# A streaming-encoder step on one core: gathers at a closer pace in the last trunk group, expert weights in the trunk's slots, row buffers from the expansion's, and a lead of two keys

## The chip, the cores and the metric

The kernel runs on one core of a Trainium2 chip. The metric is the device time of one execution in microseconds (us), the median over runs. A profiled execution has a span, from its first to its last instruction, that is a little shorter than its time. TensorE (PE) does the matrix products, VectorE (DVE) and ScalarE (ACT) the elementwise work, GpSimd (POOL) issues the indirect gathers and some stores, and SyncE (SP) issues the other transfers. Each engine and each issuing queue works through its own instructions in a fixed order.

## The reference

One layer of a hybrid encoder runs over 1152 rows of 1024 numbers: 1024 rows of one prompt and 8 × 16 rows of sampled streams. With the rows in tiles of 128 there are nine: tile 0 holds the samples, tiles 1 to 8 the prompt.

```
h = rmsnorm(x);  z = h @ w_in                      # 1024 x 10240
branch A: gelu(u) * (tril(W_s) rmsnorm(gelu(v)) + b_s), in chunks of 128 positions
branch B: retention, 4 heads, rotary q and k, a decayed state carried from tile to tile
x = x + (sigmoid(gA) * (yA @ w_proj_a) + sigmoid(gB) * (yB @ w_proj_b)) @ w_out
t = rmsnorm(x)
q = t @ w_query                                    # 8 heads of 2 x 128
top 16 of 128 keys on each half, then the top 16 of the 256 sums: 8 x 16 = 128 experts a row
w = softmax(the 16 values)
x = x + sum over the 128 experts:  w * gelu(t . eu[expert]) * ev[expert]
y = rmsnorm(x)
```

There are 128 × 128 = 16384 experts, each with a row of 1024 numbers in `expert_u` and another in `expert_v`. All values are float32.

## The kernel before, in words

**Two ways through the expert layer.** Six of the nine tiles (0, 1, 2, 6, 7, 8, the list `GATHER`) fetch the rows of their experts. For each of the 128 expert slots of a tile, one indirect transfer brings to each of the 128 partitions the pair (u row, v row) of its own expert: 8 KB a partition, 1 MB a gather, 768 gathers in all. DVE forms the dot product with `tx` (line 794), ACT applies gelu and the weight (lines 799 and 800), and DVE adds the weighted v row to `acc` (line 804). The other three tiles (3, 4, 5, the list `DENSE`) go through all experts. For each first key `e` of 128, the 128 experts of that key give S = tT · eu[e] (line 1017), then gelu and a product with a dense weight table `pt` (line 1022, the result is `g`), then a product with ev[e] (line 1029) that accumulates over all keys in six PSUM banks `res`.

**The trunk.** The tiles pass through the trunk in three groups, [0, 1], [2, 3, 4, 5], [6, 7, 8] (`trunk`, called at lines 968 to 973). Each group takes the same 128 weight units of 512 KB, in the order of the list `order`, through `take` (lines 137 to 160). In the first two groups each unit is split into two parts for a three-product matmul. There the raw units lie partly in the row buffers `gat` described below (line 121). The last group uses units as they are, in nine slots: three buffers each of the names `wraw`, `whi` and `wlo`. A load is issued as soon as the slot's last user has been taken (`room`).

**Side work.** While the trunk is traced, two lanes of side work are traced between its steps. One lane (`prepare`) picks the top keys of a tile as soon as its group is through the trunk, and for a dense tile expands the choice into the table `pdr` in DRAM, 32 chunks a tile, through tiles `ab` and `st` of the pool `ex` (lines 844 to 896). The other (`gather_all`, `gather`) hands out gathers. Both lanes and the trunk carry a time in model units: a matmul pass over n columns counts n / 2400 (`mm_us`), a gather counts `PACE[0]`, which is 5.0 in the trunk and 3.4 in the dense stage, and the lane that is furthest behind goes next (`run_side`, `advance`). So `PACE` sets how many gathers are traced among how much trunk work. A gather may be traced only for a tile whose group has left the trunk. So tiles 0, 1 and 2 can be gathered during the trunk and tiles 6, 7 and 8 only after it.

**What sets the order.** The traced order is a priority, not the final order. A scheduler that models the engines gives each engine the first instruction in this order that is ready, so side work can move ahead of the trunk where its buffers allow. `tc.high_priority` moves the dense stage's own instructions forward against the gathers. Once each engine's order is fixed, the chip runs it in that order.

**Buffers of the gathers.** A gather takes one of five buffers `gat` in the pool `peer`. `AHEAD` is how many gathers may be queued before the oldest is dotted, three in the trunk. After the trunk, the pools of the trunk weights and the expansion are closed, and in that memory new pools open: `gx` with three more row buffers `gax` (the lead then becomes six) and `dw` with four buffers `eu` and five `ev` for the dense weights (`fetch`, lines 997 to 1002). Keys 0, 1 and 2 are fetched at the start, then key e + 3 while key e is worked on. The table of the weights is read in 16 blocks of eight keys, two buffers `pt`, at the start of each block. The product with ev of key e − 1 follows S of key e: a lead of one key.

**The end.** After the last key the three dense tiles add `res` to their rows, normalise and store (lines 1038 to 1046), and the lane of gathers runs to its end.

Of the kernel before, what the change touches and what calls it, by code (L numbers as in the profile page):

```python
# [8 lines left out]
F32 = mybir.dt.float32  # L9
# [4 lines left out]
AF = mybir.ActivationFunctionType  # L14
# [34 lines left out]
EC = 4  # L49
LT = 16  # L50
BE = 8

@with_exitstack
def step_kernel(ctx: ExitStack, tc: tile.TileContext, x, state, wall, wst, bs, rows, vec, cst, smp, cosd, sind, euv,
# [4 lines left out]
    dr = ctx.enter_context(tc.tile_pool(name="dr", bufs=1, space=bass.MemoryType.DRAM))  # L61
    peer = ctx.enter_context(tc.tile_pool(name="peer", bufs=1))
    act = ctx.enter_context(tc.tile_pool(name="act", bufs=1))
    trunk_sb, trunk_ps = ExitStack(), ExitStack()
    wp = trunk_sb.enter_context(tc.tile_pool(name="wp", bufs=2))
    gp = trunk_ps.enter_context(tc.tile_pool(name="gp", bufs=2, space=bass.MemoryType.PSUM))
    sp = trunk_ps.enter_context(tc.tile_pool(name="sp", bufs=4, space=bass.MemoryType.PSUM))

# [25 lines left out]
    for g in range(len(GROUPS)):  # L94
# [10 lines left out]
            order += [U_IN + 2 * (32 + cb), U_IN + 2 * (32 + cb) + 1, U_PA + 2 * cb, U_PA + 2 * cb + 1]  # L105
        order += [U_OUT + i for i in range(8)] + [U_Q + i for i in range(16)]
    per = len(order) // len(GROUPS)
    NRAW, NPART, NBK = 3, 3, 2
    GB = 5
    MIX = 3  # L110
# [26 lines left out]
    def take():  # L137

        n = wst_["take"]
        wst_["take"] += 1  # L140
        while wst_["split"] < min(n + 3, plain_from):
            s = wst_["split"]
            while wst_["load"] < min(s + n_raw(wst_["load"]), plain_from):
                l = wst_["load"]
                raws[l] = load(l)
                wst_["load"] += 1
            parts[s] = [wp.tile([P, 4, 256], F32R, name=n, bufs=NPART) for n in ("whi", "wlo")]
            for r in homes[1:]:
                rings[r].append(s)
            split(parts[s], raws.pop(s))  # L150
            wst_["split"] += 1
        if wst_["split"] == plain_from:
            while wst_["load"] < len(order) and room(wst_["load"], n):
                l = wst_["load"]
                t = wp.tile([P, 4, 256], F32, name=homes[l % 3], bufs=NPART)
                nc.sync.dma_start(t, wall[order[l]])
                rings[homes[l % 3]].append(l)
                parts[l] = [t]
                wst_["load"] += 1
        return order[n], parts.pop(n)  # L160

    def products(w, a):
        return [(w[0], a[0])] if len(a) == 1 else [(w[0], a[0]), (w[1], a[0]), (w[0], a[1])]
# [474 lines left out]
    def query(gi, pl, tl, nt, T, tT, rs, unit):  # L638
        def scores(h, qh):
            for i, t in enumerate(tl):  # L640
                ps = sp.tile([P, 2, P], F32, name="sps")
                for c in range(2):
                    mm(ps[:, c], qh[:, c, i * P:(i + 1) * P], sk[c], start=True, stop=True)
                st = pl.tile([P, 2, P], F32, name="st", bufs=2 * nt)
                nc.scalar.activation(st, ps, AF.Copy, scale=rs[:, i:i + 1])
                st = st.rearrange("p a b -> p (a b)")
                if t in EARLY:
                    top_keys(t, h, st)
                else:
                    store(ssp[t][:, h], st, 1)  # L650

        prev = None
        ahead = front(gi + 1, pl) if gi + 1 < len(GROUPS) else turn_dense(pl)
        next(ahead, None)
        for h in range(PH):
            qh = pl.tile([P, 2, T], F32, name="qh", bufs=2)
            unit = unit or gemm_f(tT, T, U_Q + 2 * h)
            nc.scalar.copy(qh, (yield from unit))
            unit = None
            if prev:  # L660
                scores(*prev)
            if h > 1:
                next(ahead, None)
            prev = (h, qh)
            yield 0.5 * nt
        scores(*prev)
        yield 0.5 * nt
        for _ in ahead:
            pass


    AHEAD = [3]
    more = []
    PACE = [5.0]
    BOOST = [100]
    AB = 2
# [112 lines left out]

    queue, rows_ = [], []  # L790

    def dot(t, j, b):
        d = T_[t]
        nc.vector.tensor_tensor_reduce(out=b[:, :D], in0=b[:, :D], in1=d["x"], op0=OP.mult, op1=OP.add,  # L794
                                       scale=1.0, scalar=0.0, accum_out=d["s"][:, j:j + 1])
# [6 lines left out]
    def add(t, j, b):  # L802
        d = T_[t]
        nc.vector.scalar_tensor_tensor(d["acc"], b[:, D:], d["s"][:, j:j + 1], d["acc"], op0=OP.mult, op1=OP.add)  # L804
        if j == HK - 1:
            tmp = more[0].tile([P, 2 * D], F32, name="jn") if more else peer.tile([P, 2 * D], F32, name="gat", bufs=GB)
            out_norm(d["acc"], tmp, t)
            del T_[t]

# [16 lines left out]
    def gather(t):  # L826
        d = T_[t]
        d["x"] = peer.tile([P, D], F32, name="tx")
        nc.sync.dma_start(d["x"], tsp[t])
        d["acc"] = peer.tile([P, D], F32, name="acc", bufs=2)  # L830
        nc.sync.dma_start(d["acc"], xsp[t])
        for j in range(HK):
            rows_.append(j)
            if more and len(rows_) % (GB + more[1]) >= GB:
                b = more[0].tile([P, 2 * D], F32, name="gax", bufs=more[1])
            else:
                b = peer.tile([P, 2 * D], F32, name="gat", bufs=GB)
            nc.gpsimd.indirect_dma_start(out=b, out_offset=None, in_=euv,  # L838
                                         in_offset=bass.IndirectOffsetOnAxis(ap=d["idx"][:, j:j + 1], axis=0))
            queue.insert(0, (t, j, b))  # L840
            gathered()
            yield PACE[0]
# [54 lines left out]

    def out_norm(acc, tmp, t):

        nc.sync.dma_start(tmp[:, D:], row_bcast(rows, 2))  # L900
        final_norm(acc, tmp[:, :D], tmp[:, D:], t)

    def final_norm(acc, junk, g, t):
        r = peer.tile([P, 1], F32, name="rfin", bufs=2)
# [7 lines left out]
    def prepare():  # L912

        left, wait = list(GATHER), list(DENSE)
        while left or wait:
# [5 lines left out]
            elif due is not None:  # L921
                yield from chain(topk_units("p", due), expand(due))
                wait.remove(due)
                expanded.add(due)
            else:
                yield None

# [36 lines left out]
        flush()  # L964
        run_side(tm)

    ex_sb = ExitStack()
    for gi in range(len(GROUPS)):
        if gi == len(GROUPS) - 1:
            ex = ex_sb.enter_context(tc.tile_pool(name="ex", bufs=1))  # L970
        for c in trunk(gi):
            advance(c)
        ready.update(GROUPS[gi])
# [3 lines left out]
    while len(expanded) < len(DENSE):  # L977
        tm += 1.0
        run_side(tm)
    dense_sb = ExitStack()  # L980
    wd = dense_sb.enter_context(tc.tile_pool(name="dw", bufs=1, side="right"))
    ex_sb.close()
    trunk_sb.close()
    trunk_ps.close()
    GX = 3
    gx = ctx.enter_context(tc.tile_pool(name="gx", bufs=1))
    dp = dense_sb.enter_context(tc.tile_pool(name="dp", bufs=1))
    dps = ctx.enter_context(tc.tile_pool(name="dps", bufs=1, space=bass.MemoryType.PSUM))
    more.extend([gx, GX])
    AHEAD[0] += GX  # L990

    outs = [(n, j) for j in range(2) for n in range(len(DENSE))]
    res = {o: dps.tile([P, 512], F32, name=f"res{o[0]}{o[1]}") for o in outs}
    eu, ev, G = {}, {}, {}
    pt = None

    def fetch(e):
        if e < NKEYS:
            eu[e] = wd.tile([P, D], F32, name="eu", bufs=4)
            nc.sync.dma_start(eu[e], eud[e].rearrange("p k e -> p (k e)"))  # L1000
            ev[e] = wd.tile([P, D], F32, name="ev", bufs=5)
            nc.sync.dma_start(ev[e], evd[e])

    PACE[0] = 3.4
    hp = ExitStack()
    hp.enter_context(tc.high_priority(DP))
    for e in range(3):
        fetch(e)
    for e in range(NKEYS + 1):
        if e < NKEYS:  # L1010
            if e % BE == 0:
                pt = dp.tile([P, TD // LT, BE, LT], F32, name="pt", bufs=2)
                nc.sync.dma_start(pt.rearrange("p c e t -> p c (e t)"), pdr[e // BE])
            ps = dps.tile([P, TD], F32, name="S", bufs=2)
            w = eu.pop(e)
            for k in range(KD):
                mm(ps, w[:, k * P:(k + 1) * P], tT[:, k], start=k == 0, stop=k == KD - 1)  # L1017
            fetch(e + 3)
            a = G[e] = dp.tile([P, TD], F32, name="g", bufs=4)
            nc.scalar.activation(a, ps, AF.Gelu_apprx_tanh)  # L1020
            r16 = lambda z: z.rearrange("p (c t) -> p c t", t=LT)
            nc.vector.tensor_tensor(r16(a), r16(a), pt[:, :, e % BE], op=OP.mult)  # L1022
            hp.close()
            advance(8 * 4 * mm_us(TD))
            hp.enter_context(tc.high_priority(DP))
        if e:
            g, w = G.pop(e - 1), ev.pop(e - 1)
            for n, j in outs:
                mm(res[n, j], g[:, n * P:(n + 1) * P], w[:, 512 * j:512 * j + 512], start=e == 1, stop=e == NKEYS)  # L1029
            hp.close()  # L1030
            advance(len(outs) * 4 * mm_us(512))
            hp.enter_context(tc.high_priority(DP))
    hp.close()
    dense_sb.close()
    dz = ctx.enter_context(tc.tile_pool(name="dz", bufs=len(DENSE)))
    grow = dz.tile([P, D], F32, name="grow", bufs=1)
# [92 lines left out]
```

## Time and profile before

| | us |
|---|---|
| median of 3 runs | 3996.11 (3987.49 to 3996.43) |
| the profiled execution | 3993.61 |
| its span | 3991.9 |
| PE busy | 3564.0 (89%) |
| DVE busy | 3095.6 (78%) |
| POOL busy | 1139.9 (29%) |
| DMA | 1291.31 MB, 323 GB/s over the span |

The views give times from the span's start. A window row holds the window and its length, then busy time and number of instructions of each engine, the granted clock of PE as a share of full speed, the mean busy share of the 16 DMA engines and what they moved. A row of the timeline holds the start, the length, engine, line, operation, output and inputs with their shapes, the number of merged instructions, and in brackets how long the engine had been idle and what ended this. A group's row holds the count, the busy time, the mean in ns, the idle time before, and what ended most of it. A matmul of float32 shows as two records, so a dense key has 28: sixteen of S and twelve of `res`. A transfer's row holds its count, its size and the median time from issue to landing.

### The profile page before, as it was taken

To read this page: it belongs to the slowest core of one execution; us is meant where nothing else is said; L and a number is where in the kernel's file an instruction comes from. 1 tells how busy PE (TensorE), PEld (TensorE's weight loads), DVE (VectorE), ACT (ScalarE), POOL (GpSimd) and SP (SyncE) were. 2 spreads that over 40 slices of the span, in tenths; PEclk is the share of its full clock that TensorE was granted. 3 is DMA by queue.
4 is the path that set the end of the run, shared out by engine and by line. 5 is a ranking of instruction groups with operands and counts; after the bars stand their busy time and mean duration, and the time that the engine had idled before them with its cause. 6 is when DMAs were issued, how large, how long until landed. Compare 5 with 4: busy or idle time off the path is not lost. (4 is left out here: it accounts for less than half of the span.)

```text
span 3991.9 us, 45577 instructions
## 1 busy us (share of the span) xinstructions
PE 3564.0 (89%) x15681; PEld 2456.4 (62%) x15681; DVE 3095.6 (78%) x5859; ACT 1364.9 (34%) x3291; POOL 1139.9 (29%) x812
## 2 busy tenths in 40 slices
PE   8999999999998889988999969989999999999930
PEld 6789978787888766766586734444444444444410
DVE  5566799999898789898731269989777777777777
ACT  4445634444434425556351212121111211121121
POOL 0000013333333311323200014444333343443443
PEclk9999999999999999999999989999999999999965
DMA  8766548999988976979743469999999999999997
GB/s 313 262 222 197 174 167 350 365 354 336 366 327 340 352 266 205 359 261 358 269 143 123 151 246 414 418 388 418 418 419 419 400 418 418 418 419 418 418 362 265
DMA packets 257817, 1291.31 MB, mean 323 GB/s; under 512 B 28336, under 2 KB 43440, under 8 KB 157232
## 3 DMA queue, kind: packets, MB, share of 16 engines
q0 software_dynamic: 121472, 847.30, 53.8%
q1 hardware_dynamic: 136112, 441.08, 29.8%
q8 instruction: 124, 2.03, 0.2%
q14 instruction: 109, 0.89, 0.1%
HBM read 1221.16 MB, written 67.11 MB: 323 GB/s over the span
## 5 line engine op out<-in xcount | busy, mean ns | idle before, releaser
L838 POOL DMA_INDIRECT gat<-in_euv_dram,idx x588 | 838.7, 1426 | 1738.8 <-DVE acc L804 1089.7
L804 DVE SCALAR_TENSOR_TENSOR acc<-gat,sdot,acc 128x1024 f32<-128x1024 f32 x588 | 752.1, 1279 | 107.3 <-ACT sdot L800 103.1
L794 DVE CUSTOM_DVE_ANT_0 gat<-gat,tx 128x1024 f32<-128x1024 f32 x588 | 716.3, 1219 | 151.7 <-DMA gat<-in_euv_dram,idx 124.5
L1029 PE MATMUL res<-ev,g 128*128 128x512 f32 x1536 | 741.6, 612 | 100.3 <-DVE g L1022 100.1
L799 ACT ACTIVATE sdot<-sdot 128x1 f32<-128x1 f32 x768 | 154.6, 203 | 1781.4 <-DVE sdot L794 1779.9
L1017 PE MATMUL S<-h,eu 128*128 128x384 f32 x2048 | 724.0, 491 | 36.0 <-issue 29.6
L1017 PEld LDWEIGHTS S<-h,eu 128*128 128x128 f32 x2048 | 393.1, 192 | 383.8 <-issue 192.9
L1029 PEld LDWEIGHTS res<-ev,g 128*128 128x128 f32 x1536 | 293.6, 195 | 434.8 <-issue 223.3
L214 PE MATMUL gps<-whi,h 128*128 128x256 f32 x2688 | 518.3, 300 | 2.9 <-issue 1.2
L214 PEld LDWEIGHTS gps<-whi,h 128*128 128x128 f32 x2688 | 437.3, 193 | 23.4 <-issue 11.8
L838 POOL DMA_INDIRECT gax<-in_euv_dram,idx x180 | 259.8, 1443 | 602.6 <-DVE acc L804 299.8
L214 PE MATMUL gps<-wlo,h 128*128 128x256 f32 x1536 | 417.9, 310 | 4.4 <-DVE wlo L228 3.0
L198 PE MATMUL gps<-h,whi 128*128 128x256 f32 (+2 forms) x1520 | 405.6, 364 | 1.3 <-ACT whi L222 1.2
L198 PE MATMUL gps<-y,whi 128*128 128x256 f32 (+2 forms) x1168 | 308.8, 360 | 7.8 <-DVE y L228 3.0
L214 PEld LDWEIGHTS gps<-wlo,h 128*128 128x128 f32 x1536 | 294.7, 193 | 22.0 <-issue 9.0
L198 PEld LDWEIGHTS gps<-h,whi 128*128 128x128 f32 x1520 | 269.9, 192 | 57.6 <-ACT whi L222 1.4
L198 PE MATMUL gps<-h,wlo 128*128 128x256 f32 (+2 forms) x864 | 293.3, 379 | 6.7 <-DVE wlo L228 6.5
L804 DVE SCALAR_TENSOR_TENSOR acc<-gax,sdot,acc 128x1024 f32<-128x1024 f32 x180 | 230.7, 1282 | 61.8 <-ACT sdot L800 59.1
L794 DVE CUSTOM_DVE_ANT_0 gax<-gax,tx 128x1024 f32<-128x1024 f32 x180 | 219.9, 1222 | 44.3 <-DMA gax<-in_euv_dram,idx 43.4
L198 PEld LDWEIGHTS gps<-y,whi 128*128 128x128 f32 x1168 | 205.3, 192 | 49.9 <-DVE y L228 3.4
L228 DVE TENSOR_TENSOR wlo<-wraw,whi 128x1024 fp32r<-128x1024 f32 x172 | 209.2, 1216 | 30.8 <-ACT whi L222 30.5
L222 ACT CAST whi<-wraw 128x1024 fp32r<-128x1024 f32 x172 | 179.9, 1046 | 154.0 <-PE gps L198 91.9
(220 smaller groups left out, 4411.1 us busy)
## 6 DMA issues: line engine op xcount, KB each, us to landing
wraw<-in_wall_dram SPq DMA_DIRECT2D x214, 512.0 KB, 6.2
eu<-in_eud_dram SPq DMA_DIRECT2D x128, 512.0 KB, 8.1
ev<-in_evd_dram SPq DMA_DIRECT2D x128, 512.0 KB, 9.9
gat<-in_wall_dram SPq DMA_DIRECT2D x84, 512.0 KB, 4.7
pdr<-st POOLq DMA_DIRECT2D x24, 1024.0 KB, 6.9
pt<-pdr SPq DMA_DIRECT2D x16, 1536.0 KB, 10.8
wlo<-in_wall_dram SPq DMA_DIRECT2D x43, 512.0 KB, 4.7
whi<-in_wall_dram SPq DMA_DIRECT2D x43, 512.0 KB, 5.1
```

The source lines that it names most:

```text
L198: mm(ps[:, c, :T], x, y, start=kh == 0 and k == 0 and j == 0, stop=kh == nk - 1 and k == 3 and j == len(pr) - 1)
L214: mm(ps[:, i], y, x, start=kh == 0 and k == 0 and j == 0 and i % 2 == 0, stop=kh == 1 and k == 3 and j == len(pr) - 1 and last)
L222: nc.scalar.copy(parts[0], src)
L228: nc.vector.tensor_tensor(parts[1], src, parts[0].bitcast(F32), op=OP.subtract)
L794: nc.vector.tensor_tensor_reduce(out=b[:, :D], in0=b[:, :D], in1=d["x"], op0=OP.mult, op1=OP.add, scale=1.0, scalar=0.0, accum_out=d["s"][ ...
L799: nc.scalar.activation(d["s"][:, j:j + 1], d["s"][:, j:j + 1], AF.Gelu_apprx_tanh)
L804: nc.vector.scalar_tensor_tensor(d["acc"], b[:, D:], d["s"][:, j:j + 1], d["acc"], op0=OP.mult, op1=OP.add)
L838: nc.gpsimd.indirect_dma_start(out=b, out_offset=None, in_=euv, in_offset=bass.IndirectOffsetOnAxis(ap=d["idx"][:, j:j + 1], axis=0))
L1017: mm(ps, w[:, k * P:(k + 1) * P], tT[:, k], start=k == 0, stop=k == KD - 1)
L1029: mm(res[n, j], g[:, n * P:(n + 1) * P], w[:, 512 * j:512 * j + 512], start=e == 1, stop=e == NKEYS)
```

## The change

- The list of weight units goes on after the trunk: for 130 steps, unit ("u", e) for each key and unit ("v", e − 2) two steps later. `take` loads them through the same nine slots as the last trunk group's units. The pool `wp` stays open to the end, and `dw`, `eu`, `ev` and `fetch` are gone.
- `PACE` is 3.2 instead of 5.0 from the start of the last trunk group.
- When the last dense tile is expanded, the two buffers `st` of the expansion (8 KB a partition, as a gather's) join the five `gat` as row buffers, and `AHEAD` goes from 3 to 5. After the trunk one `gax` joins instead of three, and `AHEAD` is 6, as before. The scratch of a tile's last step is taken from `ab` and no longer from a row buffer or `jn`.
- The first block `pt` gets a pool of its own, opened in the last query stage, and is loaded from head 4 on if all is expanded, or after the trunk otherwise. Later blocks are loaded four keys ahead, in turns in two pools.
- The two PSUM tiles `S` are allocated ahead of the six `res`.
- The product with ev runs two keys behind S in place of one.

```
+LEAD = 2
...
+    for e in range(NKEYS + LEAD):
+        order += [("u", e)] * (e < NKEYS) + [("v", e - LEAD)] * (e >= LEAD)
...
-                nc.sync.dma_start(t, wall[order[l]])
+                nc.sync.dma_start(t, unit_of(l))
...
+    def unit_of(l):
+        if l < per * len(GROUPS):
+            return wall[order[l]]
+        kind, e = order[l]
+        if kind == "u":
+            return eud[e].rearrange("p (a k) e -> p a (k e)", a=4)
+        return evd[e].rearrange("p (k e) -> p k e", k=4)
...
+            if gi == len(GROUPS) - 1 and h >= 4 and not pts and len(expanded) == len(DENSE):
+                load_pt(pp[0], 0)
...
+    rings_ = [(peer, "gat", GB)] * GB
...
-            if more and len(rows_) % (GB + more[1]) >= GB:
-                b = more[0].tile([P, 2 * D], F32, name="gax", bufs=more[1])
-            else:
-                b = peer.tile([P, 2 * D], F32, name="gat", bufs=GB)
+            pool, name, bufs = rings_[len(rows_) % len(rings_)]
+            b = pool.tile([P, 2 * D], F32, name=name, bufs=bufs)
...
+                if not wait:
+                    rings_.extend([(ex, "st", 2)] * 2)
+                    AHEAD[0] += 2
...
         if gi == len(GROUPS) - 1:
-            ex = ex_sb.enter_context(tc.tile_pool(name="ex", bufs=1))
+            ex = ctx.enter_context(tc.tile_pool(name="ex", bufs=1))
+            PACE[0] = 3.2
...
-    more.extend([gx, GX])
-    AHEAD[0] += GX
+    rings_.append((gx, "gax", 1))
+    AHEAD[0] += 1
...
+    for e in range(2):
+        Ss[e] = dps.tile([P, TD], F32, name="S", bufs=2)
...
+    for e in range(NKEYS + LEAD):
         if e < NKEYS:
+            with tc.high_priority(DP):
+                if e % BE == BE // 2 and e // BE + 1 < NKEYS // BE:
+                    load_pt(pp[0] if e // BE % 2 else dp, e // BE + 1)
...
+                u, (w,) = take()
...
+        if e >= LEAD:
+            with tc.high_priority(DP):
+                u, (w,) = take()
...
+                g = G.pop(e - LEAD)
```

More of the change, by code (lines that the diff above doesn't have):

```diff
@@ L63, in step_kernel @@
     act = ctx.enter_context(tc.tile_pool(name="act", bufs=1))
-    trunk_sb, trunk_ps = ExitStack(), ExitStack()
-    wp = trunk_sb.enter_context(tc.tile_pool(name="wp", bufs=2))
+    trunk_ps, dense_sb = ExitStack(), ExitStack()
+    wp = ctx.enter_context(tc.tile_pool(name="wp", bufs=2))
     gp = trunk_ps.enter_context(tc.tile_pool(name="gp", bufs=2, space=bass.MemoryType.PSUM))
@@ L650, in scores @@
                     store(ssp[t][:, h], st, 1)
+        if gi == len(GROUPS) - 1:
+            pp.append(dense_sb.enter_context(tc.tile_pool(name="pp", bufs=1, side="right")))
         prev = None
@@ L669, in query, with load_pt @@
             pass
+    pp, pts = [], []
+    def load_pt(pool, n):
+        pts.append(pool.tile([P, TD // LT, BE, LT], F32, name="pt"))
+        nc.sync.dma_start(pts[-1].rearrange("p c e t -> p c (e t)"), pdr[n])
     AHEAD = [3]
-    more = []
     PACE = [5.0]
@@ L805, in add @@
         if j == HK - 1:
-            tmp = more[0].tile([P, 2 * D], F32, name="jn") if more else peer.tile([P, 2 * D], F32, name="gat", bufs=GB)
+            if len(rings_) > GB:
+                tmp = [ex.tile([P, D], F32, name="ab", bufs=AB) for _ in range(2)]
+            else:
+                tmp = peer.tile([P, 2, D], F32, name="gat", bufs=GB)
+                tmp = [tmp[:, 0], tmp[:, 1]]
             out_norm(d["acc"], tmp, t)
@@ L898, in out_norm @@
     def out_norm(acc, tmp, t):
-        nc.sync.dma_start(tmp[:, D:], row_bcast(rows, 2))
-        final_norm(acc, tmp[:, :D], tmp[:, D:], t)
+        nc.sync.dma_start(tmp[1], row_bcast(rows, 2))
+        final_norm(acc, tmp[0], tmp[1], t)
     def final_norm(acc, junk, g, t):
@@ L965, in advance @@
         run_side(tm)
-    ex_sb = ExitStack()
     for gi in range(len(GROUPS)):
         if gi == len(GROUPS) - 1:
-            ex = ex_sb.enter_context(tc.tile_pool(name="ex", bufs=1))
+            ex = ctx.enter_context(tc.tile_pool(name="ex", bufs=1))
+            PACE[0] = 3.2
         for c in trunk(gi):
@@ L979, in step_kernel @@
         run_side(tm)
[L980 to L983, printed above, removed]
     trunk_ps.close()
-    GX = 3
+    if not pts:
+        load_pt(pp[0], 0)
+    dg = ctx.enter_context(tc.tile_pool(name="dg", bufs=1))
     gx = ctx.enter_context(tc.tile_pool(name="gx", bufs=1))
@@ L988, in step_kernel @@
     dps = ctx.enter_context(tc.tile_pool(name="dps", bufs=1, space=bass.MemoryType.PSUM))
-    more.extend([gx, GX])
-    AHEAD[0] += GX
+    rings_.append((gx, "gax", 1))
+    AHEAD[0] += 1
     outs = [(n, j) for j in range(2) for n in range(len(DENSE))]
+    Ss = {}
+    for e in range(2):
+        Ss[e] = dps.tile([P, TD], F32, name="S", bufs=2)
     res = {o: dps.tile([P, 512], F32, name=f"res{o[0]}{o[1]}") for o in outs}
-    eu, ev, G = {}, {}, {}
-    pt = None
-    def fetch(e):
+    G = {}
@@ L998, in fetch @@
+    PACE[0] = 3.4
+    for e in range(NKEYS + LEAD):
         if e < NKEYS:
[L999 to L1023, printed above, removed]
-            advance(8 * 4 * mm_us(TD))
[L1025 to L1030, printed above, removed]
@@ new lines, in step_kernel @@
+            with tc.high_priority(DP):
+                if e % BE == BE // 2 and e // BE + 1 < NKEYS // BE:
+                    load_pt(pp[0] if e // BE % 2 else dp, e // BE + 1)
+                if e % BE == 0 and e:
+                    pts.pop(0)
+                ps = Ss.pop(e) if e in Ss else dps.tile([P, TD], F32, name="S", bufs=2)
+                u, (w,) = take()
+                assert u == ("u", e)
+                w = w.rearrange("p a b -> p (a b)")
+                for k in range(KD):
+                    mm(ps, w[:, k * P:(k + 1) * P], tT[:, k], start=k == 0, stop=k == KD - 1)
+                a = G[e] = dg.tile([P, TD], F32, name="g", bufs=4)
+                nc.scalar.activation(a, ps, AF.Gelu_apprx_tanh)
+                r16 = lambda z: z.rearrange("p (c t) -> p c t", t=LT)
+                nc.vector.tensor_tensor(r16(a), r16(a), pts[0][:, :, e % BE], op=OP.mult)
@@ L1031, in step_kernel @@
+            advance(8 * 4 * mm_us(TD))
+        if e >= LEAD:
+            with tc.high_priority(DP):
+                u, (w,) = take()
+                assert u == ("v", e - LEAD)
+                w = w.rearrange("p a b -> p (a b)")
+                g = G.pop(e - LEAD)
+                for n, j in outs:
+                    mm(res[n, j], g[:, n * P:(n + 1) * P], w[:, 512 * j:512 * j + 512], start=e == LEAD,
+                       stop=e == NKEYS + LEAD - 1)
             advance(len(outs) * 4 * mm_us(512))
-            hp.enter_context(tc.high_priority(DP))
@@ L1033, in step_kernel @@
-    hp.close()
     dense_sb.close()
```

## Prediction

> **What bounds the kernel now.** I read the slices first, then busy time by stage, counts of gathers by stage, the waits of PE and POOL, and last the timelines at the seams. Stages (columns: window, length; busy us and instruction count of PE, PEld, DVE, ACT, POOL; granted clock; DMA share; GB/s):
>
> ```profile
> 600.00:1390.00 790.00, 741.00 (x4144) 631.64 (x4143) 718.23 (x987) 348.10 (x770) 277.83 (x189) 0.97 0.92 349
> 1420.00:1990.00 570.00, 517.93 (x2197) 370.99 (x2196) 510.32 (x1432) 289.97 (x681) 143.78 (x107) 0.95 0.77 284
> 1990.00:2329.00 339.00, 339.00 (x1442) 241.97 (x1442) 95.85 (x352) 110.61 (x255) 9.96 (x9) 1.00 0.40 127
> 2329.00:2359.00 30.00, 0.39 (x4) 0.23 (x3) 21.87 (x101) 3.61 (x10) 5.57 (x6) 0.57 0.78 292
> 2440.00:3800.00 1360.00, 1262.51 (x3320) 633.30 (x3319) 1086.75 (x1639) 254.01 (x922) 561.70 (x394) 0.98 1.01 415
> 3836.00:3992.00 156.00, 0.00 (x0) 0.00 (x0) 117.03 (x149) 34.06 (x107) 61.18 (x38) 0.51 0.77 288
> ```
>
> The dense stage (2440 to 3800) runs with the DMA engines full at 415 GB/s. The end of the last trunk group (1990 to 2329) uses 127 GB/s, with DVE busy 96 of 339 us. After the dense matmuls come 156 us of gathers alone. The gathers by stage (POOL busy and count), the gap on POOL, and the seams on PE and DVE:
>
> ```profile
> 0.00:1420.00 1420.00, 301.20 (x208) 0.97 0.80 297
> 1420.00:1990.00 570.00, 122.97 (x90) 0.95 0.77 284
> 1990.00:2329.00 339.00, 1.77 (x2) 1.00 0.40 127
> 2329.00:3836.00 1507.00, 611.30 (x433) 0.96 1.01 412
> 3836.00:3992.00 156.00, 61.18 (x38) 0.51 0.77 288
> ...
> 1959.39 1.41 POOL L838 DMA_INDIRECT gat<-in_euv_dram,idx  x1 [1.12 <-DVE acc L804]
> 2118.76 1.15 POOL L868 DMA_DIRECT2D pdr<-st  x1 [14.33 <-ACT st L866]
> 2326.92 1.00 POOL L838 DMA_INDIRECT gax<-in_euv_dram,idx  x1 [207.01 <-PE gps L198]
> ...
> 1419.72 4.36 PE L198 MATMUL gps<-h,whi 128*128 128x384 f32 x13
> 2326.48 2.84 PE L643 MATMUL sps<-vc,qh 128*128 128x128 f32 x24
> 2358.93 13.14 PE L1017 MATMUL S<-h,eu 128*128 128x384 f32 x32 [29.61 <-issue]
> 3826.23 9.07 PE L1029 MATMUL res<-ev,g 128*128 128x512 f32 x14 [4.39 <-DVE g L1022]
> ...
> 3861.51 1.28 DVE L907 SCALAR_TENSOR_TENSOR dx<-dx,rfin,grow 128x1024 f32<-128x1024 f32 x1
> 3979.38 1.28 DVE L804 SCALAR_TENSOR_TENSOR acc<-gax,sdot,acc 128x1024 f32<-128x1024 f32 x1 [0.60 <-ACT sdot L800]
> 3982.40 1.28 DVE L804 SCALAR_TENSOR_TENSOR acc<-gat,sdot,acc 128x1024 f32<-128x1024 f32 x1 [0.60 <-ACT sdot L800]
> 3986.70 1.28 DVE L907 SCALAR_TENSOR_TENSOR acc<-acc,rfin,jn 128x1024 f32<-128x1024 f32 x1
> ```
>
> Last-trunk-group matmuls run from 1419.7 to 2329.3 (909.6 us), the dense ones from 2358.9 to 3835.3 (1476.4), and the last gather tile ends at 3988. POOL issues no gather from 1961 to 2327. That agrees with the code's own units. The lane starts 19 units (one top-k) into group 1, which is 751 units long; group 2 is 728 (128 weight units of 5.12 and 73 of smaller steps). At 5.0 a gather, (732 + 728) / 5 = 292 are handed out before the trunk ends. The rows count 298 up to 1990, less one that two windows share: 297, which is 292 and five later ones into free `gat` buffers. The next need `gax`, whose memory is the trunk's, and POOL stands 207 us for it. So 471 of 768 gathers fall behind the trunk.
>
> In the dense stage two rows show how the engines hang together (the waits of PE, then clean PE keys):
>
> ```profile
> PE res L1029 <- DVE g L1022: 100.1, 67, 9.1
> ...
> 3402.44 3.39 PE L1017 MATMUL S<-h,eu 128*128 128x384 f32 x10
> 3412.75 3.39 PE L1017 MATMUL S<-h,eu 128*128 128x384 f32 x10
> 3423.06 3.39 PE L1017 MATMUL S<-h,eu 128*128 128x384 f32 x10
> ```
>
> A key costs PE 10.31 us when nothing waits, 1320 for 128 keys. The stage has 3320 / 28 = 118.6 keys in 1360 us: 11.47 us each, with 394 / 118.6 = 3.32 gathers a key. A gather is 128 rows of 8 KB, 1.049 MB. One key's traffic is 3.32 × 1.049 + 1.049 of weights + 0.197 of `pt` = 4.73 MB, or 11.4 us at 415 GB/s. So the DMA sets the key, not PE: DVE is in order, `g` stands in it behind 3.3 dots a key, and these come as fast as the rows land. I read the 100 us on `g` as this rate, not as a latency.
>
> **The change part by part.** *Gathers at 3.2 in group 2.* Handed out before the trunk's end: 732 / 5 + 728 / 3.2 = 374, and by the same overhang up to seven more (five `gat`, two `st`): 381 against 297, 84 gathers or 88 MB earlier. Room in 1990 to 2329: (415 − 127) × 339 us = 98 MB, 93 gathers. DVE time of one, by the rows below, is 2.50 us, 210 us for 84; the stretch has 339 − 96 = 243 free. Group 1 sustained 189 in 790 us, 4.2 us each; from 1961 to 2329 that rate gives 88. I take 84.
>
> ```profile
> L804 DVE SCALAR_TENSOR_TENSOR acc<-gat,sdot,acc 128x1024 f32<-128x1024 f32 x588 | 752.1, 1279 | 107.3 <-ACT sdot L800 103.1
> L794 DVE CUSTOM_DVE_ANT_0 gat<-gat,tx 128x1024 f32<-128x1024 f32 x588 | 716.3, 1219 | 151.7 <-DMA gat<-in_euv_dram,idx 124.5
> ...
> pdr<-st POOLq DMA_DIRECT2D x24, 1024.0 KB, 6.9
> pt<-pdr SPq DMA_DIRECT2D x16, 1536.0 KB, 10.8
> eu<-in_eud_dram SPq DMA_DIRECT2D x128, 512.0 KB, 8.1
> ```
>
> *What that costs the trunk.* Dots and adds now stand in DVE's queue before the trunk's own evictions, and PE waits for those. Where both ran (1420 to 1990) PE idled 52 of 570 us, 9%; in group 1, 6%. Spread over the 339 clean us this is 20 to 31 us. The bounds are 0 (all in DVE's free time) and 48 (9% and the clock of 0.95 in place of 1.00 too). I take 25: trunk end 2354. [...]
>
> *Row buffers from the expansion's `st`.* Seven buffers and a lead of five once the expansions are out. The first two wait for `pdr` stores on the same POOL queue, 6.9 us each, hidden by five `gat`. Without that cover: 14 us of POOL, which idles there anyway. In the dense stage there are eight buffers as before: no change. The final tile's scratch in `ab` and the single `gax` cost nothing while the queue holds seven others; a `gax` at the head can block POOL as in the 207 us row, but only behind the 374.
>
> *Weights through the trunk's slots, `pt` early, S banks first.* The 29.6 us on PE at the seam is the pool's release, then the first `eu` (issued at 2355). Nine slots were nine buffers before too. Each load waits on SP for the unit eight ahead of it to finish: eight units of 5.2 us (half a clean key) are 41 us of lead against 8.1 to land, and `tx`, `acc` and key loads behind it on SP wait at most one unit, 5 us, once a tile. I keep 2 of the 30 us (bounds 0 and 12, a late `pt` of 10.8): dense start 2356.
>
> *Two keys of lead.* If `g` were merely late, with waits of at most 9.1 us, this would free most of the 100 us. Since I read the wait as a rate, it gives one key's slack once: 10 us. Bounds 0 and 100.
>
> *Dense stage.* 387 gathers at 3.32 a key keep the DMA full for 116.6 keys of 11.47, 1337 us; the other 11.4 keys cost PE 10.31, 118; less 10: 1445. The 84 gathers thus shorten the stage little; they take away the tail behind it. PE ends at 3801, the gathers before it.
>
> *Tail.* From PE's end to the last `dx` norm it took 27.5 us, with gather work between; the span ended 3.9 after its last norm. Loads of `dx` may now start sooner, since they wait only for `pt`: 20 + 4 (bounds 15 and 32).
>
> **Sum:** 2329 + 25 + 2 + 1445 + 24 = 3825 of span (before 3992). The profiled execution took 3993.6, 1.7 above its span, and the median is 2.5 higher still: 3830.
>
> **Rivals.** *B, PE comes loose:* the order on DVE spreads the 387 gathers over all keys, 3.02 a key, and the lead absorbs what is left. Then traffic is 4.41 MB, 10.6 us a key, 1361 in all: 3825 − 84 = 3741, 3746 as a time. For: waits on `g` are single, short ones, and the hand-out of 3.4 against 10.24 units a key is 3.01. Against: the same hand-out stood there before, and the order came out at 3.32. *C, gathers not moved in full:* DVE, 90% busy from 1420 to 1990, takes the expansions (their last `pdr` store is now at 2119) later and half the 84 stay. 429 left at 3.32 need 129 keys, the whole stage at 11.47 (1468) and a few gathers of 3.03 us (3982.40 − 3979.38) with a norm behind: about 3860; with none moved 471, 46 of them behind: 2331 + 1468 + 46 × 3.03 + 10 + 4 = 3952. *D, slower:* DVE's queue in group 2. If the scheduler puts each dot where its rows have not landed, PE pays for the wait. At 1 us for each of the about 230 gathers of the group the trunk slips 230 us, ending at 2559 and the whole at 4034; it decides from 0.9 us a gather (a slip of about 200). For: the lane is 1.56 times denser. Against: group 1 carried a gather each 4.2 us and lost PE 49 of 790 us, 0.26 each. *E, no effect:* the scheduler, which orders by readiness, again leaves 1961 to 2327 empty because the lane stops at a buffer of a later pool, and the lost 30 us come back as stalls: 3990.
>
> **How the numbers follow.** Forecast (3780 to 3865) 55%, B 17%, C 18%, E 3%, D 7%. The range, 3735 to 3915, takes in half of B and most of C; below lies 8%, above 12%. A measurement of this kernel tells about 0.3% from no change; faster 0.90 (the forecast, B, C), same 0.03 (E), slower 0.07 (D).
>
> **What would show it.** Right: about 380 gathers issued before the trunk's last matmul, DMA above 350 GB/s from 1990 on; PE idle of about 5% there; the wait of S on "issue" gone; DMA again at about 415 with waits on `g` still some 70 us or more; the last instruction on PE's `dx` chain, not on a gather. B shows as keys of 10.6 us and waits on `g` under 30 us; C as gathers of the third tile still far into the dense stage; D as a trunk end beyond 2530. I am wrong in the main point if the dense stage takes under 1400 us.

## The result and the profile after

The changed kernel takes 3847.86 us (median of four runs, 3841.39 to 3848.43) against 3991.8 us before (four runs; the table above has the first three); the ratio is 0.9641, with a 95% interval of 0.9614 to 0.9668. The profiled execution has a span of 3846.2 us. The forecast was 3830.

Busy time by stage in the changed kernel (columns as before: window, length; busy us and count of PE, PEld, DVE, ACT, POOL; granted clock; DMA share; GB/s):

```profile
1420.00:1990.00 570.00, 515.13 (x2189) 369.37 (x2188) 520.78 (x1422) 294.75 (x692) 149.23 (x114) 0.96 0.80 291
1990.00:2200.00 210.00, 201.02 (x850) 140.98 (x849) 132.49 (x229) 92.86 (x246) 57.98 (x44) 1.00 0.80 298
2200.00:2300.00 100.00, 74.75 (x301) 57.32 (x300) 69.82 (x101) 28.15 (x90) 36.92 (x24) 0.86 0.99 404
2300.00:2375.00 75.00, 70.64 (x288) 45.97 (x287) 69.77 (x249) 24.79 (x75) 25.07 (x15) 1.00 0.94 375
2375.00:2460.00 85.00, 83.96 (x231) 43.47 (x231) 78.05 (x290) 17.60 (x37) 18.50 (x16) 1.00 0.63 240
2460.00:3700.00 1240.00, 1148.76 (x3019) 579.28 (x3018) 978.66 (x1431) 225.72 (x827) 489.23 (x354) 0.97 1.01 416
3700.00:3834.00 134.00, 126.74 (x338) 63.51 (x336) 70.01 (x92) 18.77 (x64) 21.79 (x17) 1.00 0.62 246
```

The end of the last trunk group now moves about 300 to 400 GB/s, where it moved 127. The same windows for the gathers alone (POOL):

```profile
0.00:1420.00 1420.00, 302.72 (x208) 0.97 0.81 298
1420.00:1990.00 570.00, 128.43 (x97) 0.96 0.80 291
1990.00:2375.00 385.00, 111.58 (x76) 0.96 0.88 341
2375.00:3700.00 1325.00, 507.73 (x370) 0.97 0.99 404
3700.00:3834.00 134.00, 21.79 (x17) 1.00 0.62 246
```

Up to the trunk's end there are 208 + 97 + 76 = 381 gathers, and 387 behind it. The seams (last trunk matmuls, first S, last `res` on PE; then on DVE the last add of a gather and the last norm):

```profile
2372.60 1.60 PE L655 MATMUL sps<-vc,qh 128*128 128x128 f32 x12 [0.77 <-ACT qh L672]
2374.80 2.85 PE L1039 MATMUL S<-h,wraw 128*128 128x384 f32 x8 [0.60 <-ACT st L657]
3828.18 5.31 PE L1052 MATMUL res<-wraw,g 128*128 128x512 f32 x12
...
3778.55 1.28 DVE L828 SCALAR_TENSOR_TENSOR acc<-gat,sdot,acc 128x1024 f32<-128x1024 f32 x1 [0.60 <-ACT sdot L824]
3840.99 1.28 DVE L933 SCALAR_TENSOR_TENSOR acc<-acc,rfin,ab 128x1024 f32<-128x1024 f32 x1
```

The trunk ends at 2374.2, 45 us later than before. The seam of 30 us is gone. The dense matmuls take 1459 us (1476 before) and end at 3833.5. The last gather has been added 54 us ahead of that, and 12.7 us after PE's end the span is over. Before, 156 us of gathers stood there. The last instruction is the norm of a gather tile, which stands on DVE behind the three norms of the dense tiles. PE's waits in the dense stage of the changed kernel (total, number, longest):

```profile
PE S L1039 <- ACT g L1041: 83.4, 45, 7.1
PE res L1052 <- DVE g L1043: 15.4, 4, 7.5
```

They are 99 us; before, they were 100 on `g` and 6 on ACT. For the most part they only have another name: PE now waits for ACT to empty S, and little for DVE to deliver `g`. One of these waits, with what stands ahead of it on ACT and DVE:

```profile
3409.16 1.23 DVE L818 CUSTOM_DVE_ANT_0 st<-st,tx 128x1024 f32<-128x1024 f32 x1 [0.64 <-DMA st<-in_euv_dram,idx]
3410.42 0.20 ACT L823 ACTIVATE sdot<-sdot 128x1 f32<-128x1 f32 x1 [3.23 <-DVE sdot L818]
3410.86 0.47 ACT L1041 ACTIVATE g<-S 128x384 f32<-128x384 f32 x1
3411.38 5.19 PE L1039 MATMUL S<-h,wraw 128*128 128x384 f32 x10 [3.54 <-ACT g L1041]
```

ACT's `g` stands behind a gather's `sdot`, this waits for DVE's dot, and the dot for its row.

### The profile page after: what moved, and what is told of

Its sections match the earlier page's. It is cut to its first block, busy times and chain, and to the rows that moved or that the text cites. A ratio compares the mean times of both kernels' runs of the same rounds, so it can differ in the third digit from the quotient of the medians.

```text
span 3846.2 us, 45638 instructions
## 1 busy us (share of the span) xinstructions
PE 3561.4 (93%) x15681; PEld 2459.1 (64%) x15681; DVE 3093.8 (80%) x5859; ACT 1359.5 (35%) x3288; POOL 1113.9 (29%) x812
## 5 line engine op out<-in xcount | busy, mean ns | idle before, releaser
L818 DVE CUSTOM_DVE_ANT_0 gat<-gat,tx 128x1024 f32<-128x1024 f32 x602 | 733.1, 1218 | 149.9 <-DMA gat<-in_euv_dram,idx 133.7
L828 DVE SCALAR_TENSOR_TENSOR acc<-gat,sdot,acc 128x1024 f32<-128x1024 f32 x602 | 769.8, 1279 | 102.3 <-ACT sdot L824 96.5
L1039 PE MATMUL S<-h,wraw 128*128 128x384 f32 x688 | 249.4, 500 | 32.9 <-ACT g L1041 32.3
L1039 PE MATMUL S<-h,whi 128*128 128x384 f32 x688 | 249.2, 500 | 27.2 <-ACT g L1041 27.2
L1039 PE MATMUL S<-h,wlo 128*128 128x384 f32 x672 | 239.3, 492 | 24.1 <-ACT g L1041 23.9
L1052 PE MATMUL res<-wlo,g 128*128 128x512 f32 x516 | 244.4, 601 | 8.6 <-DVE g L1043 8.6
L1052 PE MATMUL res<-wraw,g 128*128 128x512 f32 x516 | 243.3, 598 | 5.7 <-DVE g L1043 5.7
L864 POOL DMA_INDIRECT st<-in_euv_dram,idx x116 | 164.5, 1418 | 280.1 <-DVE acc L828 244.0
L1052 PE MATMUL res<-whi,g 128*128 128x512 f32 x504 | 237.5, 598 | 1.1 <-DVE g L1043 1.1
```

## The experiments

Each ratio is against the kernel before on the same chip; the changed kernel's own is 0.9641.

**The pace back at 5.0, all else of the change kept.**

```
         if gi == len(GROUPS) - 1:
             ex = ctx.enter_context(tc.tile_pool(name="ex", bufs=1))
-            PACE[0] = 3.2
```

> The changed kernel with the pace of the last trunk group back at 5.0; everything else of the change stays. Theory (moved traffic): the gathers handed out earlier are the gain. About 294 gathers come before the dense stage again, the last trunk group ends near 2331 us with POOL idle for some 300 us before it, every dense key is tied to 3.3 gathers and takes 11.5 us (1468), and some 56 gathers of 3.03 us stand behind it: about 2331 + 1468 + 170 + 10 = 3980. Rival (the new start and the lead are the gain): the time stays under 3900.

It took 3990.97 us, ratio 1.0007 (0.9997 to 1.0016). One line's instructions as PE ran them (minimum, median, longest ns; first and last start), the trunk's last and the dense stage's:

```profile
L655 PE MATMUL sps<-vc,qh x288: 270/275/582, 453.7 to 2330.0; 128*128 128x128 f32 x144
L1051 PE MATMUL res<-wraw,g x516: 592/592/1222, 2346.5 to 3802.7; 128*128 128x512 f32 x172
```

The trunk ends at 2330 again, the dense stage takes 1472 us, and 181 us follow it. So the weights in the trunk's slots, the early `pt`, the row buffers and the lead of two keys are worth nothing while 467 gathers are left behind the trunk: they start PE 28 us sooner, and the end is set by the gathers.

**The kernel before with the pace of 3.2 alone.**

```
         if gi == len(GROUPS) - 1:
             ex = ex_sb.enter_context(tc.tile_pool(name="ex", bufs=1))
+            PACE[0] = 3.2
```

> The kernel before with one edit, the pace of 3.2 in the last trunk group. Theory (moved traffic): nearly the whole gain comes from this one number. Trunk end near 2375 as in the changed kernel, then the old seam of 30 us, a dense stage of 1459 as in the changed kernel, an old tail of 30: about 3895. Rival (the parts need each other, five row buffers can't carry the closer pace): above 3950.

It took 3884.93 us, ratio 0.9736 (0.9719 to 0.9752). The same view, and PE's waits:

```profile
L643 PE MATMUL sps<-vc,qh x288: 270/275/582, 450.6 to 2377.8; 128*128 128x128 f32 x144
L1018 PE MATMUL S<-h,eu x2048: 486/486/978, 2404.1 to 3854.1; 128*128 128x384 f32 x187
L1030 PE MATMUL res<-ev,g x1536: 592/592/1222, 2417.8 to 3861.8; 128*128 128x512 f32 x192
```

```profile
PE res L1030 <- DVE g L1023: 96.5, 44, 12.1
PE S L1018 <- DVE pos L690: 26.0, 1, 26.0
```

One number gives some 104 of the 144 us. Five row buffers carry the closer pace. The trunk ends at 2378, then comes the old seam, here 26 us, a dense stage of 1458 us and an end of 19.5. The other parts of the change are worth the rest: the seam, 26 us, the end, 19.5 against 12.7, and 4 us at the trunk's end.

**A lead of one key.**

```
-LEAD = 2
+LEAD = 1
```

> The changed kernel with a lead of one key. Theory (the waits on g are a rate): PE's waits move from S behind ACT's gelu back to res behind g, the dense stage grows by about one key's slack, 10 us: about 3858. Rival (the waits are a latency that the lead hides): the dense stage grows by 70 us or more: 3915 and above.

It took 3856.11 us, ratio 0.967 (0.9654 to 0.9687). PE's waits from the seam on:

```profile
PE res L1052 <- DVE g L1043: 99.7, 51, 8.4
PE S L1039 <- ACT g L1041: 4.5, 1, 4.5
```

The total is again about 100 us, under the old name. The dense stage ran from 2370.7 to 3839.1, 1468 us: 10 us more, one key's slack. In time the two kernels are hardly to be told apart (the intervals of their ratios overlap), and the kernel before with the pace alone, which has a lead of one key too, has a dense stage of 1458 us. So the 10 us are not shown beyond this pair. The waits on `g` are no latency that a lead could hide.

**Fewer gathers a key in DVE's order.** What is traced behind the `g` of a key is also issued behind it on DVE, and the pace of the dense stage goes from 3.4 to 3.3.

```
-    PACE[0] = 3.4
+    PACE[0] = 3.3
...
-                nc.vector.tensor_tensor(r16(a), r16(a), pts[0][:, :, e % BE], op=OP.mult)
-            advance(8 * 4 * mm_us(TD))
+                gins = nc.vector.tensor_tensor(r16(a), r16(a), pts[0][:, :, e % BE], op=OP.mult)
+            with tc.issue_after(gins.ins):
+                advance(8 * 4 * mm_us(TD))
...
-            advance(len(outs) * 4 * mm_us(512))
+            with tc.issue_after(gins.ins):
+                advance(len(outs) * 4 * mm_us(512))
```

> The changed kernel with the side work traced behind each key's g also issued behind that g on DVE, and a pace of 3.3 in the dense stage: DVE's order then holds 3.1 gathers a key in place of 3.3, with the same gathers in all. Theory (order on DVE times the rows' rate sets the key): traffic a key falls to 3.1 x 1.049 + 1.246 = 4.50 MB, 10.8 us at 416 GB/s; PE's waits fall below 40 us, the dense stage takes about 1390 in place of 1459, the time is about 3775 to 3790. Rival (waits come from latency, or from DMA as such): dense stage and time within 10 us of the changed kernel.

It took 3823.78 us, ratio 0.9589 (0.9573 to 0.9605): a gain of 24 us over the changed kernel, where 58 to 73 were expected. Its dense stage by windows:

```profile
2500.00:2600.00 100.00, 93.13 (x248) 47.33 (x247) 77.36 (x99) 17.84 (x68) 38.87 (x31) 0.98 1.02 419
2900.00:3000.00 100.00, 72.80 (x183) 36.49 (x182) 80.57 (x280) 16.00 (x52) 29.21 (x19) 0.86 0.82 315
3000.00:3700.00 700.00, 674.09 (x1794) 343.91 (x1793) 532.39 (x698) 128.08 (x471) 230.22 (x202) 0.98 1.02 418
```

and the same windows of the changed kernel:

```profile
2500.00:2600.00 100.00, 79.03 (x190) 39.12 (x190) 72.14 (x155) 14.58 (x55) 34.87 (x25) 0.88 0.97 395
2900.00:3000.00 100.00, 78.39 (x187) 37.59 (x187) 76.21 (x98) 17.11 (x66) 35.23 (x28) 0.88 1.02 419
3000.00:3700.00 700.00, 666.90 (x1776) 338.32 (x1775) 532.90 (x673) 128.77 (x473) 274.14 (x203) 0.99 1.02 418
```

From 3000 to 3700 the two have 1794 / 28 = 64.1 and 63.4 keys, 10.93 and 11.04 us each, with 202 and 203 gathers, 3.15 and 3.20 a key. Their traffic at 418 GB/s, (3.15 × 1.049 + 1.246) / 0.418 = 10.89 and 11.01 us, is the measured key to 0.04. So the rate holds; while the transfers are full that is little more than bookkeeping. And in these 700 us the spread kernel is only 18 records ahead, 0.6 of a key or 7 us. The dense stage took 1418 us, 41 less than in the changed kernel, and more than half of that lies near 2500, where the changed kernel has a hole (190 records against 248, two keys fewer). DVE stood there for the scores that the top-k of a coming tile loads:

```profile
DVE v L708 <- DMA s<-ssp: 16.7, 4, 7.6
```

Near 2900 both have a hole, with PE busy 73 and 78 of 100 us. In the spread kernel's, POOL stood up to 20 us without a gather, behind the top-k of a coming tile, which I had tied to `g` as well. Its end is longer too, 32 us behind the last matmul against 12.7. So the run shows a gain, and that the holes count; it is weak evidence that fewer gathers a key make a shorter one.

**No weights to load in the dense stage.** The pair of key 0 is loaded once into two of the slots and used for all keys; the list of units ends with the trunk. The kernel leaves out the other keys' weights, so its dense tiles are not those of the layer.

```
-    for e in range(NKEYS + LEAD):
-        order += [("u", e)] * (e < NKEYS) + [("v", e - LEAD)] * (e >= LEAD)
...
+    once = [wp.tile([P, 4, 256], F32, name=n, bufs=NPART).rearrange("p a b -> p (a b)") for n in homes[:2]]
+    nc.sync.dma_start(once[0], eud[0].rearrange("p k e -> p (k e)"))
+    nc.sync.dma_start(once[1], evd[0])
```

> The changed kernel with the weights of key 0 alone loaded in the dense stage and used for every key (127 pairs of 512 KB loads left out, so the dense tiles' values differ); the same order of gathers and of g on DVE, 3.3 a key. Theory (order times rate): a key's traffic falls from 4.7 to 3.6 MB, 8.8 us at 416 GB/s, below PE's 10.31; PE's waits nearly go, the dense stage takes 1330 to 1370 in place of 1459, time about 3720 to 3760, the DMA engines no longer full. Rival (DVE and ACT hold g by their own work and latency): PE's waits of 99 us stay, time above 3820.

It took 3749.11 us, ratio 0.941 (0.9388 to 0.9432). One window of the dense stage and PE's waits:

```profile
2460.00:3700.00 1240.00, 1210.48 (x3254) 620.38 (x3253) 1023.55 (x1504) 245.35 (x886) 587.36 (x371) 0.99 0.90 338
...
PE S L1038 <- ACT g L1040: 17.4, 12, 3.1
PE res L1049 <- DVE g L1042: 12.0, 2, 7.4
```

A key takes 1240 / (3254 / 28) = 10.67 us and PE's waits fall from 99 to 29 us, with nearly the same order on DVE and more gathers a window. The DMA engines are busy 0.90 of it instead of 1.01. DVE and ACT have the same work as before, so the wait on `g` was not theirs: this is the most direct evidence that it was a wait for transfers. It does not tell their bytes from their number, since both fell.

**The two `st` buffers, and with them the longer queue of gathers, only after the trunk.**

```
                 if not wait:
-                    rings_.extend([(ex, "st", 2)] * 2)
-                    AHEAD[0] += 2
+                    pass
...
-    rings_.append((gx, "gax", 1))
-    AHEAD[0] += 1
+    rings_.extend([(ex, "st", 2)] * 2)
+    rings_.append((gx, "gax", 1))
+    AHEAD[0] += 3
```

> The changed kernel with the two st buffers and the larger lead given to the gathers after the trunk only (five buffers and a lead of three to its end). Theory (the trunk's slip of 46 us comes from the added DVE work and rows in front of the trunk's evictions): the trunk ends at about 2375 again, same time within 10 us. Rival (seven rows in flight fill the DMA engines and delay the trunk's weights and evictions from 2200 on): trunk end 15 to 25 us earlier, time about 3825 to 3835.

It took 3856.24 us, ratio 0.9675 (0.9657 to 0.9694), and the trunk ended at 2384.1, ten us later than in the changed kernel:

```profile
L655 PE MATMUL sps<-vc,qh x288: 270/275/582, 453.0 to 2383.9; 128*128 128x128 f32 x144
```

The trunk's last 80 us in that kernel, by windows:

```profile
2300.00:2380.00 80.00, 73.18 (x284) 48.06 (x285) 39.59 (x213) 16.98 (x39) 0.00 (x0) 0.94 0.46 155
```

So the trunk's slip doesn't come from seven rows in flight. The last 80 us of the trunk have no gather issued at all here. All 381 were issued by 2285, and the next goes into `gax`, for which POOL stands until the trunk is over:

```profile
2397.43 0.94 POOL L864 DMA_INDIRECT gax<-in_euv_dram,idx  x1 [112.39 <-DVE iu L712]
```

By the times, the row buffers are worth some 8 us; the intervals of the two ratios (0.9657 to 0.9694 here, 0.9614 to 0.9668 for the changed kernel) overlap, so this is not clear of the noise.

**A pace of 3.7.**

```
-            PACE[0] = 3.2
+            PACE[0] = 3.7
```

> The changed kernel with a pace of 3.7 in the last trunk group: about 350 gathers before the dense stage, 418 in it. Theory (a knee at 3.28 gathers for each of 128 keys, 420): the gathers then just end with the keys, every key takes 11.5 us (1470), and the trunk slips less, by about 30 us: 2360 + 1470 + 14 = 3845, no worse than the changed kernel by more than 15. Rival (each gather moved is worth the same): 26 of the some 80 moved gathers are given back, a third of the gain, about 3890.

It took 3847.04 us, ratio 0.966 (0.9639 to 0.9681): not to be told from the changed kernel.

```profile
L655 PE MATMUL sps<-vc,qh x288: 270/275/583, 452.5 to 2359.4; 128*128 128x128 f32 x144
L1052 PE MATMUL res<-wraw,g x516: 592/592/1222, 2375.8 to 3826.3; 128*128 128x512 f32 x172
```

DVE's order has 357 gathers ahead of the first `g` here, against 381 at 3.2 and 301 at 5.0. The trunk ends at 2359.7, the gathers end with the keys. So the last 24 gathers moved bring nothing: what the dense stage saves, the trunk pays. By the trunk's ends at the three paces (2330.3, 2359.7, 2374.2) a gather moved costs it (2359.7 − 2330.3) / 56 = 0.53 us and (2374.2 − 2330.3) / 80 = 0.55.

**Only the lane of gathers issued behind `g`, with two pairs of paces.** As the spread kernel, but top-k runs free; first with 3.2 in the trunk and 3.25 in the dense stage, then with 3.5 and 3.3.

```
+                elif behind:
+                    with tc.issue_after(behind[-1].ins):
+                        c = next(lane[1])
                 else:
                     c = next(lane[1])
...
+                behind.append(nc.vector.tensor_tensor(r16(a), r16(a), pts[0][:, :, e % BE], op=OP.mult))
```

> As the spread kernel, but only the lane of gathers is issued behind each key's g (the top-k of the next tiles is free to run ahead), with a dense pace of 3.25: 3.15 gathers a key on DVE, 4 behind the last key. Theory: the hole at the change of tiles (POOL idle for 20 us behind top-k near 2900, PE busy 73 of 100 us there) shrinks, the time falls by 5 to 15 below the spread kernel: 3808 to 3820. Rival (the hole is the top-k's own DVE work, wherever it stands): within 5 of 3824.

> As the kernel with only the lane of gathers behind g, with paces of 3.5 in the last trunk group and 3.3 in the dense stage: some 20 gathers fewer before the dense stage, 30 behind its last key. Theory: the trunk slips some 8 us less, but with 3.1 gathers a key the 30 left over stand behind the keys at 2.5 to 3 us each: 60 to 75 us slower than the spread kernel, about 3885. Rival (what stands behind is made up by a faster dense stage): below 3840.

The first took 3802.25 us, ratio 0.9523 (0.9504 to 0.9542), the best of the kernels here that do the whole layer, and beat its expectation. Two of its windows:

```profile
2500.00:2600.00 100.00, 88.65 (x227) 44.75 (x226) 80.41 (x150) 16.85 (x65) 42.35 (x30) 0.95 1.02 418
2900.00:3000.00 100.00, 88.73 (x232) 45.35 (x231) 69.93 (x95) 22.16 (x68) 35.37 (x26) 0.95 0.94 383
```

The hole near 2900 shrank against the spread kernel (PE busy 89 against 73 us), but near 2500 PE lost (89 against 93), and the dense stage as a whole took 1418 us, as there. By the profiled executions, the first kernel's being the slowest of its four runs, the trunk ended 9 us later and only 15 us followed the last matmul, against 32. Behind the last `g` stood 3 gathers, against 9. So the gain that the profile shows lies in the end, and the pace was changed too; what freeing top-k is worth by itself is not shown.

The second took 3851.01 us, ratio 0.9646 (0.9627 to 0.9665), between what the two theories said. Its PE ended sooner than the spread kernel's, at 3776 against 3786, but 83 us followed it, most of them with gathers, against 32. I had priced the tail and forgotten that fewer gathers a key also end the keys sooner.

## Why the prediction was right, point by point

**What bounds the kernel.** Right. The dense key is set by the bytes that the order ties to it. Two runs say so from two sides: bytes taken away (waits 99 to 29 us), and a lead of one key (the wait only changes its name). The spread kernel's keys fit, but prove little. What I hadn't seen is that the tie runs through ACT's order as well as DVE's: with two keys of lead the waits on `g` fell to 15 us, which I had named as a sign of the rival, and the rest went to ACT. The rival, that the lead sets PE loose, fell all the same: the key stayed at 11.5 us, and its forecast of 3746 was missed by 100 us. Three smaller signs failed too. The transfers moved 341 GB/s from 1990 to 2375 and not 350, PE idled 10% there and not 5%, and the last instruction is a gather tile's norm.

**Gathers moved.** Right to the gather: 381 ahead of the trunk's end, 374 from the code's units and seven more into free buffers. The same seven stand on top of the 350 and 294 that I expected at the two other paces.

**The trunk's slip.** The term that was sized too small: 25 us forecast, bounds 0 and 48, measured 45. From 1990 to the trunk's end it took 385 us in place of 339: PE idled 38.6 of them, and it was busy 346.4 us with nearly the same matmuls, 7.4 more. I had spread the older idle share over the free stretch. PE lost little where its work is a row of short evictions (9 us from 1990 to 2200) and much where one long chain runs through DVE and ACT, from 2200 to 2300, 25 of 100 us. PE's waits from 1990 to 2375 of the changed kernel:

```profile
PE sps L655 <- ACT qh L672: 11.2, 2, 10.4
PE sps L619 <- DVE x L634: 8.7, 1, 8.7
PE gps L226 <- ACT h L236: 5.8, 1, 5.8
```

From the last line up, these are the turn from gating to projection, the first residual add, and the first query head. The turn's 5.8 us are what I had in mind: its work stood behind three dots on DVE. The two longer waits are another thing. In both, DVE itself stood for a transfer:

```profile
2229.45 0.95 DVE L634 TENSOR_TENSOR x<-x,gps 128x768 f32<-128x768 f32 x1 [9.41 <-DMA x<-in_x_dram]
2287.41 1.28 DVE L644 SCALAR_TENSOR_TENSOR tt<-x,rs,grow 128x1024 f32<-128x1024 f32 x1 [12.97 <-DMA tsp<-tt]
2291.07 0.20 ACT L823 ACTIVATE sdot<-sdot 128x1 f32<-128x1 f32 x1 [16.07 <-DVE sdot L818]
2291.75 0.80 ACT L672 COPY qh<-gps 128x768 f32<-128x768 f32 x1 [0.15 <-DMA tsp<-tt]
```

The loads of the residual's rows, `x`, were issued from 2210.7 on, and DVE could go on 18.8 us later; before, this took 8.7 us, and PE had other matmuls meanwhile (busy 100 of 100 us from 2200 to 2300). The third `tt` waits until the store of an earlier one has landed; a gather's dot stands behind it on DVE, and the query head `qh` stands behind that gather's `sdot` on ACT. The landing of both from 2150 to 2330 (median), first before, then in the changed kernel:

```profile
x<-in_x_dram SPq DMA_DIRECT2D x3, 512.0 KB, 6.8
tsp<-tt SPq DMA_DIRECT2D x3, 512.0 KB, 3.8
...
x<-in_x_dram SPq DMA_DIRECT2D x3, 512.0 KB, 14.4
tsp<-tt SPq DMA_DIRECT2D x3, 512.0 KB, 13.8
```

The DMA engines are busy 0.99 of that slice; before, it was 0.39. So 19 of its 25 us hang on transfers that land late while the DMA engines are full, and not on dots in DVE's queue, as the prediction had it.

The granted clock was lower where these waits stand: 0.86 in that slice, with its three waits of 5.8 to 10.4 us, and 1.00 in its neighbours, where no wait is longer than 1.9 us. What lowered it, no run shows.

**Row buffers.** Forecast at no change; the run that gave them back later is 8 us slower, which is not clear of the noise.

**The seam.** Forecast 2 us, measured 0.6.

**The dense stage.** Forecast 1445, measured 1459. The coupled key came out at 1240 / 107.8 = 11.50 us against 11.47. That it came so close is in part luck: it is the mean of 11.04 us from 3000 on, with fewer gathers a key than I had, and of slower keys ahead of that. Keys outside the coupling were more than I had: some 8 ran at PE's own pace at the start, while the next tile's top-k was still under way, and 5 at the end. What offsets them are the two holes near 2500 and 2900. The kernel before has a shallower one near 2600 (PE busy 83 of 100 us), which I had passed over. The ten us for the lead fit the one pair of kernels that differ in it alone.

**The tail.** Forecast 24, measured 12.7, since the rows for the last norm were there and no gather was left to share DVE.

**The sum.** 2329.3 + 44.9 + 0.6 + 1458.7 + 12.7 = 3846.2 against 3825 of span: the forecast had 20 us too little for the trunk and 14 too little for the dense stage, 11 too much for the tail and 1 too much for the seam. That the total is off by 21 us only is in part luck, since the errors ran against each other. Of the others, the slower rival needed a slip of about 200 us, and 45 came. The rival that not all would be moved fell. The time of the one of no effect did come, in the kernel with the pace of 5.0, though not for its reason: no gathers were moved there, and then all other edits together are worth nothing.

What stays open is how the rest of the slip splits between DVE's time, ACT's and transfers that land later; the trace settles it for the three longest waits only, and no run took them apart.

## What to carry to other kernels

In the dense stage here, with the DMA engines busy 1.01, PE's waits on another engine's result were for the most part waits for bytes that stood ahead of it in that engine's order: without the loads of the dense weights they fell from 99 to 29 us. A lead of two keys in place of one mostly moved the name of the wait (104 us at one key, 99 at two). Count the bytes that the order ties to one step and divide by the measured rate before buying slack, and look for the stretch where the transfers idle: moving bytes there was worth more here than all else (104 of the 144 us). And the gain had a knee: once the moved bytes let the two streams end together, 24 further gathers cost about as much where they landed as they saved where they were (3847.04 us at a pace of 3.7, 3847.86 at 3.2).

## What the runs showed that I had not expected

A gather that fills idle time was not free for the stage that it entered: 0.53 to 0.55 us of trunk for 2.5 us of DVE work, at two paces alike. In the slice where the trunk lost most, the price was not that DVE work but the late landing of the trunk's own transfers (19 of 25 us). Fewer row buffers made the slip worse, not better (trunk end 2384 against 2374). And leaving top-k free, together with a slightly closer pace, was worth a further 22 us (3823.78 to 3802.25); the profiles put this at the end of the kernel, and which of the two edits did it is not shown.
